# Emitting the late output matmuls of an RWKV scan ahead of the state's own update, and the merge of the solved triangles after the pair's last gate blocks

## The chip, the core and the metric

The kernel runs on one NeuronCore of a Trainium2 chip. The metric is the device time of one execution in microseconds (us). Before the change the median of three runs is 3319.86 us (3317.98 to 3334.59). The engines named below are TensorE (PE; its weight loads are listed apart as PEld), VectorE (DVE), ScalarE (ACT), GpSimd (POOL) and SyncE (SP), which issues the DMAs. Each works off its own list of instructions in order.

## The reference

One step of a two-layer model on 128 context and 512 latent tokens of width 1024, all in float32. The part that matters here is the RWKV-7 branch of each layer: 16 heads of 64, two scan directions, a 64x64 state per head and direction. The gates and both branches are then mixed.

```
def _rwkv_step(S, inp):
    r, w, k, v, neg_kk, b = inp
    sa = jnp.einsum('dbhij,dbhj->dbhi', S, neg_kk)
    S = S * w[..., None, :] + sa[..., :, None] * b[..., None, :] + v[..., :, None] * k[..., None, :]
    return S, jnp.einsum('dbhij,dbhj->dbhi', S, r)
...
    z = h @ p['w_in'][l]
    z_rwkv, z_u, z_v, z_ga, z_gb = jnp.split(
        z, [C_RWKV, C_RWKV + D_B, C_RWKV + 2 * D_B, C_RWKV + 2 * D_B + D_MODEL], axis=-1)
...
    y_a, S_fin = rwkv_branch(z_rwkv, S0, p, l)
    y_b = chunk_mlp_branch(z_u, z_v, p, l)
    mixed = (jax.nn.sigmoid(z_ga) * y_a + jax.nn.sigmoid(z_gb) * y_b) @ p['w_out'][l]
```

## The kernel before

The 640 tokens stand in the free dimension, the 1024 channels in eight blocks of 128 partitions. A pair is two heads, which is one such block, so a layer has eight pairs. The scan is done in chunks of 64 tokens, ten to a direction.

Every large product is a block of 48 dense matmuls (`mm_block`, L111): weights and activations are split into a high and a low part (`load_w`: SP loads the raw weights, ACT makes `hi` at L101, DVE or POOL makes `lo` at L103), and three products of 128x128 by 128x320 are summed per 128 rows. Of these there are three for each pair (`krv_block`: k, r and v) and 16 gate blocks (`gate_block`), which wait for nothing of the scan and are spread over the pairs by the numbers in `SP["gn"]`: two for most pairs, one for pairs 3 and 7, and two before the first.

For each pair there is a `front` and a `back`, both generators that emit their instructions up to the next `yield`. `front(i)` builds the chunk matrices LA and BK, their products `g` (L644), and then solves 40 small triangular systems with a chain of 60 DVE instructions on the tile X (L676 and L678). After that come two last parts. In the first, DVE transposes X into XT and XN (L692, L694) and ACT copies XT into TT (L698). In the second, the merge, 40 matmuls of 32x32 (`pw`, L705), four ACT copies (L709), 40 more matmuls of 32x32 (L715) and four more copies (L718) put the off-diagonal block into TT. `front` yields 22 times in all; the merge is what runs between the 21st and the 22nd.

`back(i)` is the recurrence: ten steps, each for both directions and heads. A step reads the state with LA (L776 for the part of the output, L751 for the solve's right-hand side), ACT copies the latter into `psb` (L780), four matmuls apply the solved triangle TT (L789), ACT and DVE copy the result into SV (L790, L791), four matmuls form the new state (L795), and two DVE additions put it into SV for the next step (L803). The last four matmuls of a step's output, `y_mm` (L757), are kept in `late` and emitted in the next step. They are followed by an addition on DVE (L764) or, where a token's output is written for the first time, a copy on ACT (L766). All of the step's matmuls are of 64 or 128 rows by 64 columns; two or four of them work side by side in the array.

The program's order is not what the code says alone. The recording layer gives each instruction a priority from its place of emission; `tc.high_priority(offset=n)` lets instructions count as if they were emitted n instructions earlier. A scheduler then goes through the program with its own reckoning of when things are ready, and puts on each engine's list the ready instruction of the highest priority. The engines work off those lists in order. `adv` takes the offset from the table SP: 200 for `front` ("F"), none for `back` ("B"). `run(i, n)` advances front i by up to n parts.

The functions that the change touches, and what calls them:

Of the kernel before, what the change touches and what calls it, by code (L numbers as in the profile page):

```python
# [31 lines left out]
DPAR = 27 + 16 + 16 + 8 + 8  # L32
SPLIT = (((0, NCH),), ((0, NCH),))
GORD = (((0, 4), (4, 4), (8, 2)), ((0, 4), (8, 2), (4, 4)))
SP = {'n': (3, 2, 1, 2, 2, 1, 0, 0, 3, 1), 'v': 1, 'k': 4, 'r': 7, 'kk': 7, 'F': 200, 'B': None, 't': 10, 'g0': 2, 'gn': (2, 2, 2, 1, 2, 2, 2, 1)}


def cidx(d, p):
# [3 lines left out]
def emit(tc, I, O, depth=DEPTH, mark=lambda s: None):  # L42
    nc = tc.nc
    ctx = ExitStack()
    with ctx:
# [261 lines left out]
        for l in range(depth):  # L307
# [73 lines left out]
            with tc.tile_pool(name=f"com{l}", bufs=1) as com:  # L381
# [11 lines left out]
                with tc.tile_pool(name=f"p1_{l}", bufs=1) as p1:  # L393
                    lah = p1.tile([128, 3, T], F32R, tag="lah", name="lah")
                    lal = p1.tile([128, 3, T], F32R, tag="lal", name="lal")
                    late = iter(range(16, 48 if l == 0 else 16))
# [7 lines left out]
                    for j in range(3):  # L404
# [9 lines left out]
                        t = p1.tile([128, T], F32, tag="pt", name="lz", bufs=4)  # L414
# [66 lines left out]
                    for q in range(4):  # L481
                        mod_some(0)
                        pss = [dense_ps(), dense_ps()]
                        for kb in range(4):
                            wh, wl = load_w(I["win"][l, 35 + 2 * q + kb // 2, :, (kb % 2) * 512:(kb % 2) * 512 + 512])
                            for kk in range(2):
                                k = 2 * kb + kk
# [33 lines left out]
                with tc.tile_pool(name=f"rw{l}", bufs=1) as rw:  # L521
# [199 lines left out]
                    def back(i):  # L721
# [3 lines left out]
                        for d in range(2):  # L725
                            for w0 in range(-1, NCH, 4):
                                tr = psr.tile([128, 4, 2, L], F32, tag="g", name="trv")
                                n = min(4, NCH - w0)
# [16 lines left out]
                        late = None  # L745

                        def y_state(pu, cs, us):
                            for d in range(2):
                                for h in range(2):
                                    s = slice(64 * h, 64 * h + 64)  # L750
                                    nc.tensor.matmul(pu[s, d, 3, :], SV[s, us[d], h, :], LA[d][s, cs[d], 1, :], start=False, stop=False, skip_group_check=True)  # L751

                        def y_mm(pu, cs, us):
                            for d in range(2):
                                for h in range(2):
                                    s = slice(64 * h, 64 * h + 64)
                                    nc.tensor.matmul(pu[s, d, 3, :], SV[:, us[d], h, :], GR[d][:, cs[d], h, :], start=False, stop=True, skip_group_check=True)  # L757
                            for d in range(2):
                                tok = cs[d] if d == 0 else NCH - 1 - cs[d]
                                dst = y[:, tok * L:(tok + 1) * L]  # L760
                                if d:
                                    dst = dst[:, ::-1]
                                if tok in seen:
                                    nc.vector.tensor_tensor(dst, pu[:, d, 3, :], dst, ALU.add)  # L764
                                else:
                                    nc.scalar.activation(dst, pu[:, d, 3, :], AF.Copy)  # L766
                                    seen.add(tok)

                        for p in [2, 0, 3, 1] + list(range(4, 10)):
                            cs = [cidx(d, p) for d in range(2)]  # L770
                            us = [cs[0], NCH + cs[1]]
                            both = slice(us[0], us[1] + 1, us[1] - us[0])
                            pu = psr.tile([128, 2, 4, L], F32, tag="pu", name="pu")
                            for d in range(2):
                                for h in range(2):
                                    nc.tensor.matmul(pu[64 * h:64 * h + 64, d, 0, :], LA[d][:, cs[d], 2 * h, :], SV[:, us[d], h, :],  # L776
                                                     start=(d == 0), stop=True, skip_group_check=True)
                            y_state(pu, cs, us)
                            psb = rw.tile([128, 2, L], F32, tag="psb", name="psb", bufs=2)
                            nc.scalar.activation(psb, pu[:, :, 0, :], AF.Copy)  # L780
                            if p != 9:
                                sw = rw.tile([128, 2, L], F32, tag="sw", name="sw", bufs=2)
                                for h in range(2):
                                    s = slice(64 * h, 64 * h + 64)
                                    nc.gpsimd.tensor_tensor(sw[s], SV[s, both, h, :], wcu[s, both].unsqueeze(2).to_broadcast([64, 2, L]), ALU.mult)  # L785
                            for d in range(2):
                                for h in range(2):
                                    s = slice(64 * h, 64 * h + 64)
                                    nc.tensor.matmul(pu[s, d, 1, :], TT[s, us[d], :], psb[s, d, :], start=False, stop=True, skip_group_check=True)  # L789
                            nc.scalar.activation(SV[0:64, both, 0, :], pu[0:64, :, 1, :], AF.Copy)  # L790
                            nc.vector.tensor_copy(SV[64:128, both, 1, :], pu[64:128, :, 1, :])  # L791
                            if p != 9:
                                for d in range(2):
                                    for h in range(2):
                                        nc.tensor.matmul(pu[64 * h:64 * h + 64, d, 2, :], BT[d][:, cs[d], h, :], SV[:, us[d], h, :], start=False, stop=True, skip_group_check=True)  # L795
                                for h in range(2):
                                    s = slice(64 * h, 64 * h + 64)
                                    if p == 1:
                                        dst = sw[s]
                                    else:  # L800
                                        v0, v1 = cidx(0, p + 1), NCH + cidx(1, p + 1)
                                        dst = SV[s, v0:v1 + 1:v1 - v0, h, :]
                                    nc.vector.tensor_tensor(dst, pu[s, :, 2, :], sw[s], ALU.add)  # L803
                                if p == 1:
                                    nc.sync.dma_start(O["st"][l, i], sw)
                            if late:
                                y_mm(*late)
                            late = (pu, cs, us)
                            yield "ch"
                        y_mm(*late)  # L810
# [23 lines left out]
                    def adv(g, what, i):  # L834
                        mark(f"{what}{i}:")
                        if SP[what] is None:
                            return next(g, None)
                        with tc.high_priority(offset=SP[what]):
                            return next(g, None)
# [13 lines left out]
                    def gate(n):  # L853
                        nonlocal gi
                        for _ in range(min(n, len(gates) - gi)):
                            mark("gate")
                            gate_block(*gates[gi])
                            gi += 1

                    def run(i, n=99):  # L860
                        f = fronts.get(i)
                        for _ in range(n):
                            if f is None or adv(f, "F", i) is None:
                                break

                    def branch_b():
# [27 lines left out]
                    for i in range(NPAIR):  # L894
                        ng = SP["gn"][i]
                        for step in range(10):
                            adv(b, "B", i)
                            run(i + 1, SP["n"][step])
                            if step == SP["v"]:
                                krv(i + 1, 2)  # L900
                            if step == SP["k"]:
                                krv(i + 2, 0)
                            if step == SP["r"]:
                                krv(i + 2, 1)
                            if step == SP["kk"]:
                                run(i + 2, 1)
                        gate(min(ng, 1))
                        if i == NPAIR - 1:
                            ya = new_acts()
                            for j in range(NPAIR - 1):  # L910
                                t = ftmp("ya")
                                nc.sync.dma_start(t, yd[j])
                                split(ya[0][:, j], ya[1][:, j], t)
                        drain(b, "B", i)
                        if i == NPAIR - 1:
                            branch_b()
                        gate(ng - 1)
                        run(i + 1)
                        if i + 1 < NPAIR:
                            b = back(i + 1)  # L920
                            adv(b, "B", i + 1)
                        run(i + 2, 4)

                mark("p3")
                with tc.tile_pool(name=f"x{l}", bufs=1) as xpool:
# [38 lines left out]
                    with tc.tile_pool(name=f"ff{l}", bufs=1) as ff:  # L964
# [3 lines left out]
                        for half in range(2):  # L968
                            fh = ff.tile([128, 16, T], F32R, tag="fh", name="fh")
                            fl_ = ff.tile([128, 16, T], F32R, tag="fl", name="fl")  # L970
                            for m in range(16):
# [6 lines left out]
                                t = ff.tile([128, T], F32, tag="nt", name="relu", bufs=3)  # L978
# [99 lines left out]
```

## Time and profile before

| | |
|---|---|
| median of three runs | 3319.86 us |
| profiled execution | 3320.89 us |
| its span, from the first to the last instruction | 3319.2 us |
| PE busy in the span | 3129.1 us (94%) |
| DVE busy | 2156.9 us (65%) |
| ACT busy | 1509.4 us (45%) |
| mean granted TensorE clock | 0.954 of 2.4 GHz |

The two stretches with the recurrence are 340 to 1055 us (layer 0) and 1960 to 2690 us (layer 1). PE is busy in most of both, DVE in four fifths. In a view of PE's timeline a row merges equal instructions that follow each other; a float32 matmul is listed as two passes, so the 40 `pw` matmuls of the program stand as x80, and a group of four state matmuls as x8. A dense matmul (L111) is listed once. The duration of a row reaches to the modelled end of its last matmul, which lies beyond the start of the next; the time that a matmul takes from PE is read from one start to the next.

### The profile page before, as it was taken

How to read it: one execution, taken by the hardware profiler on the slowest of the kernel's cores; microseconds unless marked ns; L12 is line 12 of the kernel's file. 1: busy time of each engine (PE TensorE's matmuls, PEld its weight loads, DVE VectorE, ACT ScalarE, POOL GpSimd, SP SyncE). 2: the span in 40 equal slices, each digit the busy share in tenths (PEclk: the TensorE clock that was granted, in tenths of full speed). 3: DMA queues.
4: the chain of work that ended last, by engine and by line, in shares of the span. 5: the costliest groups of instructions: out<-in, count | busy, mean ns of one | idle time of the engine just before them, and what ended most of it. 6: DMA issues, size and time to landing. Idle time of an engine off the chain costs nothing.

```text
span 3319.2 us, 66348 instructions
## 1 busy us (share of the span) xinstructions
PE 3129.1 (94%) x26160; PEld 2840.5 (86%) x26160; DVE 2156.9 (65%) x4147; ACT 1509.4 (45%) x3268; POOL 613.5 (18%) x616
## 2 busy tenths in 40 slices
PE   8999799999999999999999979999999999999998
PEld 7988677777778989999999967787777799899998
DVE  6777778878875468943363387788897735532334
ACT  5444444554555345224264434455554533541432
POOL 3004333333331010000010143333333200100000
PEclk7998889999999999999999989899999999999999
DMA  6683122222224626632344521122222345222223
GB/s 206 203 299 124 57 74 67 76 67 74 67 80 125 216 83 212 217 115 77 93 146 145 189 79 57 58 81 72 78 75 73 104 142 169 89 77 74 77 74 102
DMA packets 215671, 372.73 MB, mean 112 GB/s; under 512 B 63680, under 2 KB 72000, under 8 KB 215360
## 3 DMA queue, kind: packets, MB, share of 16 engines
q1 hardware_dynamic: 215360, 368.49, 34.7%
q8 instruction: 206, 3.38, 0.4%
q14 instruction: 105, 0.86, 0.1%
HBM read 288.41 MB, written 63.31 MB: 106 GB/s over the span
## 4 chain that ended last, share of the span: by engine, by line
PE 66%; DVE 18%; issue 5%; DMA 4%; ACT 4%; POOL 2%; SPq 0%; DVEq 0%; POOLq 0%; ACTq 0%
PE dps L111 43%; PE g L644 4%; DMA wada<-in_wada 3%; PE dps L491 3%; PE dps L256 3%; DVE D L676 2%; DVE X L678 2%; DVE wjunk L168 2%; PE pu L776 2%; PE pu L789 2%; PE pu L751 1%; PE pu L757 1%; PE pu L795 1%; DVE lo L103 1%; DVE XN L694 1%
## 5 line engine op out<-in xcount | busy, mean ns | idle before, releaser
L101 ACT ACTIVATE hi<-raw 128x512 fp32r<-128x512 f32 x630 | 396.2, 631 | 1006.6 <-PE dps L111 803.0
L103 DVE TENSOR_TENSOR lo<-raw,hi 128x512 fp32r<-128x512 f32 x550 | 393.9, 718 | 522.5 <-ACT hi L101 510.8
L111 PE MATMUL dps<-ah,hi 128*128 128x320 f32 x2768 | 685.2, 324 | 7.6 <-ACT up L468 4.1
L111 PE MATMUL dps<-ah,lo 128*128 128x320 f32 x2768 | 677.7, 321 | 0.0
L111 PE MATMUL dps<-al,hi 128*128 128x320 f32 x2768 | 677.6, 322 | 0.0
L111 PEld LDWEIGHTS dps<-ah,hi 128*128 128x128 f32 x2768 | 474.5, 192 | 26.7 <-ACT up L468 5.2
L111 PEld LDWEIGHTS dps<-ah,lo 128*128 128x128 f32 x2768 | 474.2, 192 | 14.5 <-issue 0.4
L111 PEld LDWEIGHTS dps<-al,hi 128*128 128x128 f32 x2768 | 475.0, 192 | 13.2 <-issue 0.4
L168 DVE CUSTOM_DVE_ANT_0 wjunk<-wada,sc 128x1024 f32<-128x1024 f32 x176 | 221.9, 1261 | 34.2 <-DMA wada<-in_wada 32.2
L785 POOL TENSOR_TENSOR sw<-SV,wc 64x128 f32<-64x128 f32 x288 | 150.6, 523 | 450.5 <-DVE SV L803 438.6
L644 PE MATMUL g<-LA,BK 64*128 64x128 f32 x1280 | 183.1, 315 | 34.2 <-POOL BK L625 13.4
L103 POOL TENSOR_TENSOR lo<-raw,hi 128x512 fp32r<-128x512 f32 x80 | 118.2, 1477 | 511.8 <-ACT hi L101 425.5
L111 PE MATMUL dps<-fh,lo 128*128 128x320 f32 x896 | 204.6, 310 | 3.4 <-DVE lo L103 3.4
L644 PEld LDWEIGHTS g<-LA,BK 64*128 64x128 f32 x1280 | 153.4, 211 | 62.2 <-issue 23.6
L111 PE MATMUL dps<-fh,hi 128*128 128x320 f32 x896 | 204.3, 309 | 0.0
L111 PE MATMUL dps<-fl,hi 128*128 128x320 f32 x896 | 204.1, 309 | 0.0
L676 DVE TENSOR_TENSOR D<-AA,X 128x30 f32<-128x30 f32 (+14 forms) x480 | 182.6, 380 | 24.3 <-POOL X L671 14.2
L678 DVE TENSOR_TENSOR X<-X,D 128x30 f32<-128x30 f32 (+14 forms) x480 | 176.3, 367 | 10.5
L249 POOL TENSOR_TENSOR al<-nt,ah 128x320 fp32r<-128x320 f32 x24 | 26.7, 1114 | 705.1 <-ACT ah L248 704.0
L625 POOL TENSOR_TENSOR BK<-ta,cum 64x640 f32<-64x640 f32 x64 | 128.3, 2004 | 139.2 <-DVE ta L616 108.3
L111 PEld LDWEIGHTS dps<-fh,lo 128*128 128x128 f32 x896 | 149.6, 188 | 4.7 <-DVE lo L103 4.7
L111 PEld LDWEIGHTS dps<-fl,hi 128*128 128x128 f32 x896 | 149.9, 188 | 0.0
(293 smaller groups left out, 5773.8 us busy)
## 6 DMA issues: line engine op xcount, KB each, us to landing
raw<-in_w SPq DMA_DIRECT2D x280, 256.0 KB, 2.6
raw<-in_win SPq DMA_DIRECT2D x234, 256.0 KB, 2.8
wada<-in_wada SPq DMA_DIRECT2D x88, 512.0 KB, 4.1
ld<-up SPq DMA_DIRECT2D x80, 320.0 KB, 3.5
th<-ld SPq DMA_DIRECT2D x32, 320.0 KB, 3.0
ta<-ld SPq DMA_DIRECT2D x32, 320.0 KB, 3.1
gd<-spill SPq DMA_DIRECT2D x32, 320.0 KB, 2.3
raw<-in_wo SPq DMA_DIRECT2D x40, 256.0 KB, 2.6
```

The source lines that it names most:

```text
L101: nc.scalar.activation(hi, raw, AF.Copy)
L103: (eng or nc.vector).tensor_tensor(lo, raw, hi.bitcast(F32), ALU.subtract)
L111: nc.tensor.matmul(ps[:, n, 0:HT], w[:, k * 128:(k + 1) * 128], xk[:, n * HT:(n + 1) * HT], start=(first and k == 0 and j == 0), stop=(las ...
L168: nc.vector.tensor_tensor_reduce(junk, wt, sc_cur[0][:, v, :], 1.0, 0.0, ALU.mult, ALU.add, mods[l][:, j, v:v + 1])
L256: nc.tensor.matmul(ps[:, n, 0:HT], w[:, k * 128:(k + 1) * 128], x[:, 4 * kb + k, hs(n)], start=(kb == 0 and k == 0 and j == 0), stop=(kb = ...
L491: nc.tensor.matmul(o, x[:, k, tk * 128:(tk + 1) * 128], w[:, kk * 256:(kk + 1) * 256], start=(k == 0 and j == 0 and tk % 2 == 0), stop=(k ...
L625: nc.gpsimd.tensor_tensor(b[s, c, 1 - h, :], rt[s], e[s], ALU.mult)
L644: nc.tensor.matmul(gs[h][:, c - c0, :], b[s, c, :, :].rearrange("p x t -> p (x t)"), la[s, c, h:h + 2, :].rearrange("p x t -> p (x t)"), s ...
L676: nc.vector.tensor_tensor(t3, AA[:, s + 1:32, s:s + 1].to_broadcast([128, n, s]), X[:, s:s + 1, 0:s].to_broadcast([128, n, s]), ALU.mult)
L678: nc.vector.tensor_tensor(X[:, s + 1:32, 0:s], X[:, s + 1:32, 0:s], t3, ALU.add)
L776: nc.tensor.matmul(pu[64 * h:64 * h + 64, d, 0, :], LA[d][:, cs[d], 2 * h, :], SV[:, us[d], h, :], start=(d == 0), stop=True, skip_group_c ...
L785: nc.gpsimd.tensor_tensor(sw[s], SV[s, both, h, :], wcu[s, both].unsqueeze(2).to_broadcast([64, 2, L]), ALU.mult)
```

## The change

Two edits. The call of `y_mm` for the step before moves from the end of a step to the place right behind `y_state`, ahead of the copy into `psb`. And at the end of a pair the first of the two last parts of the next front (transposes and copies) is emitted ahead of the pair's last gate blocks, still with an offset of 200, and the merge behind them, with a new offset of 60. No instruction is added or taken away on any engine: all five lists keep their counts by operation and shape.

```
-SP = {'n': (3, 2, 1, 2, 2, 1, 0, 0, 3, 1), 'v': 1, 'k': 4, 'r': 7, 'kk': 7, 'F': 200, 'B': None, 't': 10, 'g0': 2, 'gn': (2, 2, 2, 1, 2, 2, 2, 1)}
+SP = {'n': (3, 2, 1, 2, 2, 1, 0, 0, 3, 1), 'v': 1, 'k': 4, 'r': 7, 'kk': 7, 'F': 200, 'M': 60, 'B': None, 't': 10, 'g0': 2, 'gn': (2, 2, 2, 1, 2, 2, 2, 1)}
...
                             y_state(pu, cs, us)
+                            if late:
+                                y_mm(*late)
                             psb = rw.tile([128, 2, L], F32, tag="psb", name="psb", bufs=2)
...
                                     nc.sync.dma_start(O["st"][l, i], sw)
-                            if late:
-                                y_mm(*late)
                             late = (pu, cs, us)
...
-                    def run(i, n=99):
+                    def run(i, n=99, what="F"):
                         f = fronts.get(i)
                         for _ in range(n):
-                            if f is None or adv(f, "F", i) is None:
+                            if f is None or adv(f, what, i) is None:
...
                             branch_b()
+                        run(i + 1, 1)
                         gate(ng - 1)
-                        run(i + 1)
+                        run(i + 1, 9, "M")
                         if i + 1 < NPAIR:
```

The scheduler makes the following of it. On PE in layer 0, the merge of front 3 stood before as one run of 40 `pw` matmuls and then the second 40 in two runs, with state matmuls between them:

```order
L111 MATMUL dps<-al,hi 128x320
L705 MATMUL pw<-XN,TT_3559 32x32 x40
L776 MATMUL pu<-SV,LA_2793 64x64 x2
L776 MATMUL pu<-SV,LA_2815 64x64 x2
L751 MATMUL pu<-LA_2793,SV 64x64 x2
L751 MATMUL pu<-LA_2815,SV 64x64 x2
L757 MATMUL pu<-GR_2832,SV 64x64 x2
L757 MATMUL pu<-GR_2890,SV 64x64 x2
L111 MATMUL dps<-al,hi 128x320
L111 MATMUL dps<-ah,lo 128x320 x2
L715 MATMUL pw_6709<-XT,XN 32x32 x19
```

The same merge in the changed kernel, again on PE:

```order
L111 MATMUL dps<-al,hi 128x320 x2
L705 MATMUL pw<-XN,TT_3559 32x32 x16
L578 MATMUL pg<-YD,ones_b 128x320 x2
L705 MATMUL pw<-XN,TT_3559 32x32
L111 MATMUL dps<-ah,lo 128x320
L705 MATMUL pw<-XN,TT_3559 32x32
L111 MATMUL dps<-ah,lo 128x320
L705 MATMUL pw<-XN,TT_3559 32x32
L111 MATMUL dps<-ah,hi 128x320
L705 MATMUL pw<-XN,TT_3559 32x32
L111 MATMUL dps<-ah,hi 128x320
L111 MATMUL dps<-al,hi 128x320
```

After the first 16 the `pw` matmuls stand one at a time between dense matmuls; the first 40 of this merge are now in 23 pieces and the second 40 in 15.

The first edit shows on PE where a step stands among a `front`'s products. The piece is the difference between the two lists in layer 0, among the first steps of pair 0 (matmuls of L795 have the number L797 in the changed kernel):

```order
 L644 MATMUL g<-LA_3520,BK_3521 128x128 x4
-L795 MATMUL pu<-SV,BK_2794 64x64
-L795 MATMUL pu<-SV,BK_2816 64x64 x2
 L757 MATMUL pu<-GR_2832,SV 64x64 x2
 L757 MATMUL pu<-GR_2890,SV 64x64 x2
+L797 MATMUL pu<-SV,BK_2794 64x64
+L797 MATMUL pu<-SV,BK_2816 64x64 x2
```

The four output matmuls now stand ahead of the last three matmuls of the new state.

## Rows read from the trace of the kernel before

**Rows 1.** The page: busy time by engine, and the chain by engine.
```profile
PE 3129.1 (94%) x26160; PEld 2840.5 (86%) x26160; DVE 2156.9 (65%) x4147; ACT 1509.4 (45%) x3268; POOL 613.5 (18%) x616
...
PE 66%; DVE 18%; issue 5%; DMA 4%; ACT 4%; POOL 2%; SPq 0%; DVEq 0%; POOLq 0%; ACTq 0%
```
**Rows 2.** Windows of both recurrences: us, busy by engine, PEclk, DMA share, GB/s.
```profile
340.00:1055.00 715.00, 662.77 (x6962) 539.19 (x6963) 576.80 (x1229) 363.47 (x952) 239.87 (x246) 0.93 0.25 76
...
1960.00:2690.00 730.00, 674.69 (x7114) 548.79 (x7112) 589.28 (x1256) 368.78 (x961) 237.02 (x248) 0.94 0.25 76
```
**Rows 3.** PE's waits, whole span: total us, times, longest.
```profile
PE pw L705 <- DVE XN L694: 52.5, 16, 16.5
```
**Rows 4.** PE's waits, 440 to 1055 us (layer 0, fronts 1 to 7).
```profile
PE pw L705 <- DVE XN L694: 9.7, 7, 3.4
PE g L644 <- POOL wc L610: 3.5, 1, 3.5
PE g L644 <- DVE LA L656: 2.9, 5, 1.0
...
PE g L644 <- POOL BK L625: 2.0, 2, 1.4
```
**Rows 5.** PE's waits, 2060 to 2690 us (layer 1), those for `g`.
```profile
PE g L644 <- DVE LA L656: 4.5, 7, 1.3
...
PE g L644 <- POOL wc L610: 2.3, 1, 2.3
...
PE g L644 <- POOL BK L625: 1.2, 2, 1.0
```
**Rows 6.** PE's timeline around the merge of front 3, layer 0: start us, us.
```profile
630.40 0.46 PE L111 MATMUL dps<-ah,hi 128*128 128x320 f32 x2
...
632.46 0.31 PE L111 MATMUL dps<-al,hi 128*128 128x320 f32 x1
634.00 1.45 PE L705 MATMUL pw<-XN,TT 32*32 32x32 f32 x80 [1.23 <-DVE XN L694]
...
638.28 0.88 PE L715 MATMUL pw<-XT,XN 32*32 32x32 f32 x42
```
**Rows 7.** The same timeline, cut to single instructions at two borders.
```profile
636.92 0.31 PE L111 MATMUL dps<-ah,lo 128*128 128x320 f32 x1
637.16 0.31 PE L715 MATMUL pw<-XT,XN 32*32 32x32 f32 x8
...
638.97 0.19 PE L715 MATMUL pw<-XT,XN 32*32 32x32 f32 x1
639.09 0.41 PE L111 MATMUL dps<-ah,hi 128*128 128x320 f32 x1
```
**Rows 8.** PE's timeline in a step of pair 0, layer 0.
```profile
421.90 0.31 PE L111 MATMUL dps<-al,hi 128*128 128x320 f32 x1
422.14 0.33 PE L776 MATMUL pu<-SV,LA 128*64 128x64 f32 x2
422.40 0.42 PE L111 MATMUL dps<-al,hi 128*128 128x320 f32 x1
...
427.04 0.70 PE L578 MATMUL pg<-kksq,ones_b 128*128 128x320 f32 x2
427.34 0.55 PE L111 MATMUL dps<-ah,lo 128*128 128x320 f32 x1
```
**Rows 9.** PE's window behind the wait of front 2, layer 0: busy, PEclk.
```profile
555.20:558.60 3.40, 3.40 (x49) 0.50 0.51 153
```
**Rows 10.** PE's timeline in that window.
```profile
555.29 0.73 PE L111 MATMUL dps<-ah,hi 128*128 128x320 f32 x2
555.82 0.73 PE L111 MATMUL dps<-al,hi 128*128 128x320 f32 x2
```
**Rows 11.** ACT's copies on the recurrence: duration ns min/median/max.
```profile
L766 ACT ACTIVATE YD<-pu x160: 197/224/245, 394.2 to 2669.2; 128x64 f32<-128x64 f32 x160
...
L780 ACT ACTIVATE psb<-pu x160: 250/278/283, 384.8 to 2683.0; 128x128 f32<-128x128 f32 x160
```

## The prediction

> **What bounds the kernel now.** I read the busy times first. PE is busy 94% of the span and makes up 66% of the chain that ended last [rows 1], so what PE does more, or waits less, is worth about its own time as long as nothing else takes over. The change touches the two recurrences alone, and so the windows of these came next: PE is busy 662.8 of 715 us and 674.7 of 730 us there, DVE 577 and 589 [rows 2]. PE is the fuller engine, and DVE has a fifth to spare. Then PE's waits, to see what the change could take away: the longest group is the merge's first matmul (L705) waiting for DVE's second transpose, 52.5 us in 16 waits [rows 3]. Of these 9.7 us are those of fronts 1 to 7 in layer 0 [rows 4], and layer 1 shows the same sum. The other 33.1 us belong to the first front of each layer, which has no gate blocks in the place that the change uses. So the second edit can win 19.4 us of waiting at most. Last I compared PE's two lists, since a wait that goes is replaced by what stands there instead.
>
> **The first edit.** It adds nothing; the four output matmuls, the addition and the copy of each step only move. On PE they stood directly behind L751, where the edit asks for them, in 84 of 160 steps before, and do in 92 after; behind the state's update (L795) they stood in 36 and stand in 28. The scheduler had filled this place already, and I cost the edit on PE at nothing; what hides it are the dense matmuls around each step. On ACT it adds a wait. In 28 steps, against 6 before, a copy of the output (L766) now stands right ahead of the copy into `psb` (L780), and that waits for two copies of 0.224 us [rows 11] and for the output matmuls before them. Behind `psb` come TT's matmuls (L789). 22 steps by 0.45 us is 10 us on the recurrence's own chain, but a dense matmul or two stand ahead of L789 in each step, as in the step shown [rows 8]. I take 2 us. No DMA is moved by it.
>
> **The second edit, what it takes away.** The wait at the merge goes only if PE has more to do ahead of it. For front 1 of layer 0, whose wait is the longest, 3.4 us [rows 4], 64 dense matmuls stood between the last group-norm product (L578) and the merge; now it is 59, at 0.147 us each (14 starts from 630.40 to 632.46 [rows 6]). For front 2 the count from there falls from 41 to 19, with two more L578 among them, while DVE has three products fewer and one half of the group norm more ahead of the transposes. For front 3 the merge moves behind the step's end on both engines. The scheduler believes XN ready sooner than it is, in both kernels, and puts the merge where it believes so. I take 5 of the 19.4 us as won, with 0 and 19.4 as the ends.
>
> **The second edit, what it adds.** With the offset of 60 the merge's matmuls have nearly the priority of the dense ones beside them, and the list takes them in turn. The first 40 of the 16 merges stood in 16 pieces and now stand in 202; the second 40 went from 20 pieces to 108. Counting over PE's whole list, it goes from matmuls that fill the array (128 rows by 128 columns) to smaller ones and back 639 times before and 871 times after: 232 more.
>
> The price of one such visit is in the trace. From a dense matmul to the first `pw` pass is 0.24 us (636.92 to 637.16), from the last pass back to a dense one 0.12 us (638.97 to 639.09) [rows 7], and a pass within a run takes 0.017 us (638.28 to 638.97 for 41 [rows 6, 7]). A lone `pw`, two passes, thus takes 0.24 + 0.017 + 0.12 = 0.377 us from one dense matmul to the next, where 0.147 us would pass without it and 0.034 us is what it costs within a run. That leaves 0.196 us for each visit, and 232 of them make 45.5 us. From below, an instruction of another line between dense ones that fills the array costs nothing but its passes: L578 takes 0.30 us for two passes of 320 columns, 0.006 us over two dense ones. From above, a lone L776 takes 0.50 us from dense to dense, 0.35 over [rows 8]. The ends are 1 and 82 us. I take 45.5, since the borders priced are those of these very instructions.
>
> The Trainium skill, on its page "TensorEngine Tiling (Array Packing)", section "Tiling Modes" (Key Properties), says that changing the tiling mode drains the engine; the 0.24 and 0.12 us agree. The same page, section "Performance Considerations" (Instruction Overhead), gives a matmul about 60 cycles of overhead; if that were all, my estimate at 2.4 GHz would be 232 x 0.025 = 6 us, and the sum would end 39.5 us lower, at 3313 us.
>
> What hides a part of it: after each merge PE waits for LA, BK and `wc` of the next front before its products `g`, 8.4 us in layer 0 and 8.0 in layer 1 [rows 4, 5]. Where PE is late anyway, these waits shrink. But the exponentials on ACT that DVE and POOL need for them now stand behind copies that wait for the stretched merge (L709), as do casts of the weights (L101; four buffers of `hi` are the cover, 24 dense matmuls each). I take 10 of the 16.4 us as hidden. The gate blocks' loads and stores on SP are the same number, and no DMA stands among the releasers of PE's waits in these two lists [rows 4, 5].
>
> **Sum.** 45.5 - 10 - 5 + 2 = 32.5 us on the profiled 3320.89 us, which is 3353.4. The median of the runs shown is 1.03 us under that execution, so 3352 us.
>
> **Rivals.** About 0.5%, 17 us, is what a measurement of this kernel can tell from no change; faster means under 3303 and slower over 3336 us.
>
> A second price, the clock. Behind the wait of front 2 the granted clock is 0.50 for 3.4 us [rows 9], 1.2 GHz, and a dense matmul takes 0.265 us [rows 10]. A stretch of lone matmuls gives PE little work in its time too, 232 x 0.377 = 87 us in all. If it all ran at the low level at up to 1.8 times the time, that is 70 us more; a third of it makes 23 us and 3375 us. For it speaks that the mean clock is 0.93 and 0.94 in just these two windows [rows 2]; against it, that the recurrence's steps, full of borders too, run at the full clock: the step shown enters L776 in 0.24 us [rows 8], as a dense matmul is left in rows 7.
>
> No change. The visits cost 45.5 us, but all of the waits for `g` and at the merge fill up: 45.5 + 2 - 19.4 - 16.4 = 12 us, 3331 us. The merges stand next to just these waits, which speaks for it; the lists, which put no more ahead of the merge than before, speak against it.
>
> Faster. A lone `pw` fits between dense matmuls at little over its passes, as L578 does: 1 us. The waits at the merges go (19.4), and with them four stretches like that of rows 9, 1.7 us lost in each, 7 us: 1 + 2 - 19.4 - 7 = -23, 3297 us. It decides as soon as a visit costs less than (19.4 + 7 - 2) / 232 = 0.105 us. The rule of 60 cycles cited above from the Trainium skill would lead here. Against it stand 0.24 and 0.12 us, read at those instructions. That the second edit does nothing is excluded by the lists; that the first does nothing is what I forecast.
>
> **How the numbers follow.** The forecast has a chance of 0.58, and its own range is 3337 to 3372 us (10 us hidden may be 0 to 16.4, 5 won may be 19.4, and 0.196 may be 0.25). The clock has 0.15, no change 0.17, faster 0.10. For 8 in 10 the range goes from 3316 to 3388 us, which leaves out the faster case and the clock's far end. Slower by over 0.5%: nearly all of the forecast and the clock, 0.70. Within: no change, a little of the forecast and a part of the faster case, 0.23. Faster: 0.07.
>
> **What would show it.** In the changed profile, PE's lone L705 between two L111 should take 0.37 to 0.38 us from dense to dense; if it is 0.2, the main term is wrong. PE's waits at L705 should still sum to over 40 us (33.1 of the first fronts, and most of 19.4); if under 36, the edit did win them. The waits for `g` should fall by half. The windows of the two recurrences should be 16 us longer each, and all others the same. PEclk below 0.90 in these windows would be the rival of the clock. The forecast is wrong as a whole if these windows grow by less than 5 us each.

## The result and the profile after

The changed kernel takes 3445.86 us (median of 6 runs, 3429.19 to 3459.31) where the kernel before takes 3329.81 us (6 runs, the three of its table among them): a ratio of 1.035, 95% interval 1.0319 to 1.0381. That it would be slower was forecast, the size was not: 116 us measured against 32.5 forecast, and outside the range.

The lines of the page that answer to [rows 1]:

```profile
PE 3268.5 (95%) x26160; PEld 2907.9 (85%) x26160; DVE 2160.5 (63%) x4147; ACT 1507.1 (44%) x3268; POOL 600.7 (17%) x616
...
PE 74%; DVE 14%; DMA 4%; issue 4%; ACT 3%; POOL 1%; SPq 0%; DVEq 0%; POOLq 0%; ACTq 0%
```

PE is busy for 139 us more with the same 26160 instructions, while DVE, ACT and POOL are busy about as long as before. So the same matmuls take PE longer. To find the place, each trace is read from the first matmul of a layer's first merge to that of its last. The columns are those of [rows 2]; first the kernel before, then the changed one:

```profile
369.82:1009.66 639.84, 604.99 (x6283) 491.95 (x6283) 520.97 (x1129) 322.31 (x863) 225.92 (x229) 0.94 0.23 70
1994.66:2629.68 635.02, 600.34 (x6284) 488.46 (x6284) 523.58 (x1129) 322.12 (x863) 222.26 (x229) 0.94 0.23 71
```

```profile
364.35:1056.62 692.27, 666.41 (x6245) 521.73 (x6245) 523.66 (x1127) 319.32 (x859) 217.87 (x227) 0.89 0.21 65
2047.33:2747.80 700.47, 673.92 (x6246) 523.75 (x6248) 522.90 (x1127) 319.17 (x859) 215.83 (x227) 0.88 0.21 64
```

The stretches grow by 52.4 and 65.5 us, 117.9 of the span's 121.3 (3440.5 against 3319.2). The granted clock in them falls from 0.94 to 0.89 and 0.88. PE's busy time in them grows by 61.4 and 73.6 us, 135.0 in all; its idle time, which is the rest of a stretch, falls from 69.5 us in the two to 52.4. Within them, four of the merges of layer 0 (fronts 3 to 6) from the first `pw` to the end of the second 40, PE's columns and PEclk again; before, then after:

```profile
634.00:639.09 5.09, 5.09 (x196) 4.50 (x196) 2.83 (x7) 3.76 (x10) 2.19 (x3) 1.00 0.41 119
731.68:735.90 4.22, 4.22 (x169) 3.99 (x169) 2.11 (x5) 3.16 (x8) 0.42 (x1) 1.00 0.22 58
829.91:835.90 5.99, 5.99 (x171) 5.62 (x171) 5.92 (x9) 3.80 (x9) 0.42 (x1) 0.72 0.21 59
916.67:922.10 5.43, 5.43 (x196) 4.66 (x196) 1.61 (x5) 4.39 (x11) 1.22 (x3) 1.00 0.18 61
```

```profile
633.96:663.74 29.78, 29.78 (x206) 18.31 (x206) 16.89 (x20) 9.03 (x17) 6.25 (x5) 0.69 0.09 29
743.12:761.80 18.68, 18.68 (x215) 12.55 (x215) 5.14 (x12) 5.31 (x12) 2.77 (x4) 0.63 0.25 82
847.61:868.50 20.89, 20.89 (x194) 13.55 (x194) 14.08 (x16) 9.14 (x17) 6.35 (x5) 0.73 0.06 18
945.20:981.80 36.60, 36.60 (x218) 22.39 (x216) 17.06 (x21) 8.63 (x16) 6.68 (x5) 0.65 0.19 60
```

20.7 us have become 106 us, with 833 matmul passes where there were 732, and PE is never idle in them by the profile. Much of the clock's loss is here too: 0.63 to 0.73 where the whole stretch has 0.89. Single rounds in the merge of front 3 (PE's timeline, start and length), first at the full clock and then at the low one:

```profile
636.55 0.42 PE L111 MATMUL dps<-ah,lo 128*128 128x320 f32 x1
636.89 0.24 PE L705 MATMUL pw<-XN,TT 32*32 32x32 f32 x2
637.07 0.41 PE L111 MATMUL dps<-ah,hi 128*128 128x320 f32 x1
...
653.58 0.64 PE L111 MATMUL dps<-ah,hi 128*128 128x320 f32 x1
654.15 0.31 PE L715 MATMUL pw<-XT,XN 32*32 32x32 f32 x2
654.39 0.64 PE L111 MATMUL dps<-al,hi 128*128 128x320 f32 x1
```

From dense to dense it is 0.52 us at 636.55 and 0.81 us at 653.58, where I had forecast 0.377. Last, PE's waits at the merges of fronts 1 to 7 and for the products `g`, layer 0 and then layer 1, which answer to [rows 4] and [rows 5]:

```profile
PE pw L705 <- DVE XN L694: 8.7, 6, 3.4
PE g L644 <- DVE LA L656: 4.0, 6, 1.6
...
PE g L644 <- POOL BK L625: 1.8, 2, 1.2
```

```profile
PE pw L705 <- DVE XN L694: 8.7, 6, 3.3
PE g L644 <- DVE LA L656: 4.3, 7, 1.6
...
PE g L644 <- POOL BK L625: 0.3, 1, 0.3
```

At the merges that is 17.4 us where it was 19.4: the wait that the second edit was placed to fill is still there. The waits for LA, BK and `wc` are 10.4 us where they were 16.4.

### The profile page after: what moved, and what is told of

Same layout as the page of the kernel before. It is cut to its first block, busy times and chain, and to the rows that moved or that the text cites. A ratio compares the mean times of both kernels' runs of the same rounds, so it can differ in the third digit from the quotient of the medians.

```text
span 3440.5 us, 66359 instructions
## 1 busy us (share of the span) xinstructions
PE 3268.5 (95%) x26160; PEld 2907.9 (85%) x26160; DVE 2160.5 (63%) x4147; ACT 1507.1 (44%) x3268; POOL 600.7 (17%) x616
## 4 chain that ended last, share of the span: by engine, by line
PE 74%; DVE 14%; DMA 4%; issue 4%; ACT 3%; POOL 1%; SPq 0%; DVEq 0%; POOLq 0%; ACTq 0%
PE dps L111 47%; PE g L644 4%; DMA wada<-in_wada 3%; PE dps L491 3%; PE dps L256 2%; PE pu L776 2%; DVE wjunk L168 2%; PE pu L791 2%; PE pu L757 2%; PE pw L705 2%; DVE D L676 2%; PE pg L578 2%; DVE X L678 2%; PE pu L751 1%; PE pu L797 1%
## 5 line engine op out<-in xcount | busy, mean ns | idle before, releaser
L111 PE MATMUL dps<-ah,hi 128*128 128x320 f32 x2768 | 712.5, 332 | 7.8 <-ACT up L468 4.9
L111 PE MATMUL dps<-ah,lo 128*128 128x320 f32 x2768 | 711.2, 331 | 0.0
L103 DVE TENSOR_TENSOR lo<-raw,hi 128x512 fp32r<-128x512 f32 x550 | 382.5, 697 | 510.8 <-ACT hi L101 494.3
L111 PE MATMUL dps<-al,hi 128*128 128x320 f32 x2768 | 702.7, 329 | 0.0
L111 PEld LDWEIGHTS dps<-ah,hi 128*128 128x128 f32 x2768 | 481.6, 195 | 32.4 <-ACT up L468 5.9
L111 PEld LDWEIGHTS dps<-ah,lo 128*128 128x128 f32 x2768 | 485.2, 195 | 18.0 <-issue 1.5
L111 PEld LDWEIGHTS dps<-al,hi 128*128 128x128 f32 x2768 | 482.5, 195 | 16.5 <-issue 0.6
L111 PEld LDWEIGHTS dps<-fh,hi 128*128 128x128 f32 x896 | 149.8, 188 | 0.0
```

Of the source, the lines that this page charges most:

```text
L103: (eng or nc.vector).tensor_tensor(lo, raw, hi.bitcast(F32), ALU.subtract)
L111: nc.tensor.matmul(ps[:, n, 0:HT], w[:, k * 128:(k + 1) * 128], xk[:, n * HT:(n + 1) * HT], start=(first and k == 0 and j == 0), stop=(las ...
```

## The experiments

Theory 1 was that the lost time is PE's price for going from dense matmuls to a small one and back, with the clock that falls where it does so often. Theory 2 was that the merge, and with it the next recurrence, simply comes later. Theory 3 laid it to the first edit. How late a merge comes can be counted in the traces, in passes of PE's other matmuls ahead of it, here for layer 0 (layer 1 has the same differences): against the kernel before, the change starts it later in fronts 3 and 6 only (4200 and 6452 passes, before 4141 and 6414), and ends it later in fronts 1, 3, 4, 5 and 6. Visits are counted over PE's list as in the prediction: 639 before, 871 in the changed kernel.

**The first edit alone.** The last part of a pair is put back:

```
-                        run(i + 1, 1)
                         gate(ng - 1)
-                        run(i + 1, 9, "M")
+                        run(i + 1)
```

> Only the first edit (output matmuls ahead of psb); the merge as before. PE's list has 631 visits to smaller matmuls, 8 fewer than before (639; the changed kernel has 871). Theory 1 (the time is PE's price for the extra visits, plus the clock that falls in them): ratio to before 0.995 to 1.003, and PEclk of the recurrences 0.92 or more. Theory 2 (the merge comes late and the recurrence waits for it): also about 1.00, since the merge is not moved. Theory 3 (the copies of the output that stand ahead of psb on ScalarE slow the recurrence): about 1.035, as the whole change.

Measured: 3322.95 us against 3330.04, ratio 0.9985 (0.9963 to 1.0006). Theory 3 falls: the first edit can't be told from no change.

**The second edit alone.** The call of `y_mm` is put back behind the state's update.

> Only the second edit (merge behind the gate blocks with offset 60); the output matmuls as before. 877 visits, 238 more than before. Theory 1: 238 by 0.5 us each (116 us over 232 visits in the whole change) is 119 us, ratio 1.036, and PEclk 0.87 to 0.90 in the recurrences. Theory 2: 1.035 as well. Theory 3: 1.00.

Measured: 3458.65 us, ratio 1.0394 (1.0359 to 1.0429), and 0.926 for the mean clock of the span. All of the loss is in the second edit; 128.6 us over 238 visits is 0.54 us for each.

**The merge in the change's place, but whole.** The change, with each 40 matmuls of a merge tied to the first of them. The helper `keep` issues the first as the change does and the other 39 behind it at a high priority:

```
...
+                        def keep(f):
+                            if not head:
+                                head.append(f())
+                            else:
+                                with tc.issue_after(head[0].ins), tc.high_priority(offset=1000):
+                                    f()
...
```

> The whole change, but each 40 matmuls of a merge are kept together: the first of them has the offset of 60 and its place, the other 39 follow it at a high priority. 633 visits. Theory 1: ratio 0.99 to 1.005, PEclk 0.92 or more, since all the extra visits are gone though the merge starts as late as in the change. Theory 2: 1.02 to 1.035, since the merge starts at its late place. Theory 3: 1.035.

Measured: 3334.5 us, ratio 1.0015 (0.9991 to 1.0039), mean clock 0.949. The merge starts within 29 passes of where it starts in the change, and nothing is lost. What costs is that the merge stands in pieces. For Theory 2 this run is not enough: a whole merge also ends earlier, in front 3 after 4194 other passes where it was 4246.

**No offset for the merge.** One number is changed in the changed kernel: `'M': 60` becomes `'M': None`.

> The whole change with no offset for the merge in place of 60: the merge's matmuls then stand behind nearly all of the gate block's, later than in the change, in 22 pieces each for the first and the second 40; 623 visits, 16 fewer than before. Theory 1: ratio 0.985 to 1.00 (16 visits fewer, and the first matmul of a merge waits less for the transposes). Theory 2: slower than the change, 1.035 to 1.05, since the merge is later still. Theory 3: 1.035.

Measured: 3299.12 us, ratio 0.9916 (0.9883 to 0.9949). In fronts 2 to 6 the merge starts and ends later than in the change, in few pieces, and the kernel is faster than before. Theory 2 falls here. PE's busy time and, over the whole span, the wait at the merge's first matmul and two waits of the transposes `trv` behind the merge, which load SV for the next pair:

```profile
PE 3101.2 (94%) x26160; PEld 2817.9 (86%) x26160; DVE 2157.1 (66%) x4147; ACT 1507.6 (46%) x3268; POOL 605.3 (18%) x616
...
PE pw L705 <- DVE XN L694: 39.3, 8, 16.0
...
PE trv L730 <- ACT TT L718: 13.7, 14, 2.6
PE trv L730 <- ACT SV L735: 10.0, 6, 4.4
```

At the merge that is 13.2 us less than the 52.5 of [rows 3], and 8 waits where there were 16. But the two waits of `trv` were 2.3 and 1.1 us before:

```profile
PE trv L730 <- ACT TT L718: 2.3, 6, 0.5
...
PE trv L730 <- ACT SV L735: 1.1, 7, 0.2
```

PE's idle time in the span is 192.0 us where it was 190.1, so the gain is not there; it is in the 27.9 us by which PE is busy less. 16 visits fewer are about 5 us of that at the price found below; the mean clock is 0.959 where it was 0.954, and how the rest divides is open.

**An offset between.** `'M': 100`.

> The whole change with an offset of 100 for the merge in place of 60: 767 visits, 128 more than before, where the change has 232 more. Theory 1: 128/232 of 116 us, 64 us, ratio 1.019; 1.012 to 1.027. A rival by which any offset under 200 that lets the merge mix costs the same: 1.035.

Measured: 3397.37 us against 3325.75, ratio 1.0213 (1.0189 to 1.0236). 71.6 us over 128 visits is 0.56 us for each, as in the second edit alone (0.54) and the whole change (116 over 232, 0.50). Over these three the time goes with the number of visits.

**The price by itself.** Here small matmuls are added to the kernel before, in the feed-forward part of layer 1 where PE has nothing but dense work. Their result is not used. `small` issues one, in turn in two places of the array, and stands behind every dense matmul of seven blocks:

```
+            tc.keep_in_program_order(nc.tensor.matmul(lone[0][64 * h + 32:64 * h + 64, 0:32], ident[q, 0:32], ident[q, 0:32], start=True, stop=True))
...
                             start=(first and k == 0 and j == 0), stop=(last and k == 3 and j == 2))
+                        if lone[0] is not None and n >= 0:
+                            small()
```

> The kernel before with 336 matmuls of 32x32 added in the second layer's first feed-forward half, where PE does nothing but dense matmuls: one behind every dense matmul of seven blocks. Their result is not used. Theory 1, with the durations read at the changed kernel's lone merge matmuls (0.34 us into it, 0.053 for its two passes, 0.12 out, where 0.147 would pass): 336 by 0.37 us is 124 us if the clock stays full; if it falls to the low level in that stretch, 0.81 us a round, 336 by 0.66 us, 222 us. The price as predicted (0.24 us in) would give 336 by 0.23 us, 77 us. Rival: a small matmul between dense ones costs only its passes, under 15 us, and the lost time in the changed kernel came from waits around the merge.

Measured: 3551.87 us (two runs), 226 us more, ratio 1.0677 (1.0634 to 1.0721). PE's timeline where the stretch begins and in its middle (L119 is the dense matmul here, `lone` the small one), and then windows of the stretch and of the dense work after it, with PEclk behind the five engines:

```profile
2887.52 0.41 PE L119 MATMUL dps<-ah,hi 128*128 128x320 f32 x1
2887.86 0.24 PE L111 MATMUL lone<-ident 32*32 32x32 f32 x2
2888.03 0.41 PE L119 MATMUL dps<-al,hi 128*128 128x320 f32 x1
...
3000.38 0.64 PE L119 MATMUL dps<-ah,lo 128*128 128x320 f32 x1
3000.95 0.31 PE L111 MATMUL lone<-ident 32*32 32x32 f32 x2
3001.19 0.64 PE L119 MATMUL dps<-ah,hi 128*128 128x320 f32 x1
```

```profile
2891.00:3156.00 265.00, 265.00 (x987) 152.66 (x986) 14.53 (x21) 21.94 (x33) 0.00 (x0) 0.50 0.05 14
3160.00:3300.00 140.00, 140.00 (x956) 140.00 (x956) 39.65 (x65) 39.80 (x61) 0.00 (x0) 1.00 0.24 74
```

The first rounds take 0.51 us; then the clock falls, each takes 0.81 us, and it stays low for all 265 us until the dense work after it. 336 rounds by 0.81 - 0.147 us are 223 us: there is no merge here, and PE is listed as busy for all of the 265 us, so no wait for another engine has a part in it.

The same number behind every second dense matmul (`n >= 1`, 14 blocks):

> As the run before, but the same 336 small matmuls stand behind every second dense matmul of 14 blocks; their result is not used. Theory 1: with two dense matmuls between them the way in costs 0.24 us, not 0.34, as in the trace of the kernel before: 336 by 0.27 us is 89 us at the full clock, and the clock stays full more of the time, since dense work fills more than half of the round. If the way in costs 0.34 us here too: 336 by 0.37, 124 us.

Measured: 3454.34 us (two runs), 129 us more, ratio 1.0384 (1.0345 to 1.0423). The same two views of it:

```profile
3000.17 0.56 PE L119 MATMUL dps<-ah,hi 128*128 128x320 f32 x2
3000.66 0.24 PE L111 MATMUL lone<-ident 32*32 32x32 f32 x2
3000.83 0.56 PE L119 MATMUL dps<-al,hi 128*128 128x320 f32 x2
```

```profile
2885.80:3107.00 221.20, 221.20 (x1343) 144.13 (x1342) 31.73 (x43) 49.27 (x73) 0.00 (x0) 1.00 0.11 36
```

The clock stays full. A round is 0.66 us (3000.17 to 3000.83) where two dense matmuls take 0.294: 0.37 us more, 123 us over 336 rounds. I had expected that two dense matmuls between visits make each cheaper, 89 us; they don't. The way in is 0.24 us then, but the first dense matmul after a visit takes 0.25 us instead of 0.147 (3000.17 to 3000.66 is 0.49 for both). With one dense matmul between visits the same 0.1 us shows as a way in of 0.34 us.

And 48 in a row behind each of seven blocks:

> The same 336 small matmuls as in the runs that priced them (result not used), but 48 in a row behind each of seven blocks, so 7 visits. If a visit's price lies in the way in and out: 7 by 0.33 us and 336 by 0.034 to 0.053 us, 14 to 20 us, ratio 1.004 to 1.006, and the clock stays full. If the price lies in each small matmul: over 89 us, as measured between dense ones.

Measured: 3343.42 us against 3329.28, ratio 1.0043 (1.0021 to 1.0065), 14 us for the same 336 matmuls.

```profile
2895.30 0.46 PE L119 MATMUL dps<-ah,lo 128*128 128x320 f32 x2
2895.69 1.71 PE L111 MATMUL lone<-ident 32*32 32x32 f32 x96
2897.33 0.57 PE L119 MATMUL dps<-ah,hi 128*128 128x320 f32 x2
```

From the first of 48 small matmuls to the next dense one it is 1.64 us here (2895.69 to 2897.33). The price is the visit's, not the small matmul's. Which part of a passage takes the time, the change of the array's use or the load of other weights, these runs do not separate.

**What is best.** With no offset and whole runs:

> The whole change with no offset for the merge and each 40 of its matmuls kept together. 617 visits, 22 fewer than before and 6 fewer than with no offset alone; all 32 groups of 40 in one piece. Theory 1: 6 visits by 0.5 us are 3 us: ratio 0.985 to 0.993, the same as or slightly under the run with no offset alone (0.9916). Theory 2 is out already.

Measured: 3309.36 us against 3325.75, ratio 0.9952 (0.9926 to 0.9977), faster than before but outside what I had expected; keeping the runs whole wins nothing over no offset. Then no offset again, in five more runs:

> The version with no offset once more (whole change, merge without offset), in five rounds, for its interval: ratio 0.988 to 0.995 as before. If the first result was chance, 0.995 to 1.00.

Measured: 3299.16 us against 3329.28, ratio 0.9915 (0.9884 to 0.9947). And no offset without the first edit:

> The second edit alone with no offset; the output matmuls as before. 629 visits, 10 fewer than before. If the gain of the version with no offset comes from the merge's place (its first matmul waits 8 us in fronts 1 to 7 of both layers, where it waited 19.4): 0.988 to 0.996. If it needs the first edit: 0.997 to 1.002.

Measured: 3300.0 us, ratio 0.9916 (0.9884 to 0.9948). No offset beats both kernels by itself; the first edit adds nothing that can be told. The wait at the merge's first matmul, over the whole span:

```profile
PE pw L705 <- DVE XN L694: 37.6, 6, 16.5
```

## Why the prediction was wrong

The prediction had the cause, and two terms of its second edit were wrong: the price of a visit, and the clock, which stood in the sum at nothing.

**The first edit** was costed at nothing on PE and 2 us on ACT. Measured alone it is 0.9985; right, as far as this can tell.

**The count of visits** was right as a cause: the loss follows it over four kernels (0, 128, 232 and 238 more visits, 0, 72, 116 and 129 us). Small differences do not follow it: 16 visits fewer went with 31 us less, 22 fewer with 16.

**The price of one such visit** is the first step that failed. I put it at 0.377 us from dense to dense and 0.196 us net, from the borders of a run. Those borders are right, 0.24 us in and 0.12 us out, but they are not all of a visit: the first dense matmul after one takes 0.1 us more, and a lone small matmul's own two passes 0.053 us, not the 0.017 of a run. A round takes 0.516 us at the full clock, 0.335 us net (less 0.147 and 0.034). 232 of those are 78 us where I had 45.5. [Rows 8] had shown 0.35 us for a lone state matmul, and the trace of the kernel before has 52 such rounds at the full clock, with a median of 0.35. I kept that for the upper end and trusted the cheaper reading because it was of the same instructions, though at the end of a run of 42 and not of a lone one.

**The clock** is the second step that failed, and the larger one. It was a rival with a chance of 0.15 in place of a term of the sum, and its 23 us were too little. The sign named for it, PEclk below 0.90 in the two stretches, came: 0.89 and 0.88. Of the 230 rounds in the trace with a dense matmul on both sides of a lone one, 145 ran wholly at the low level, 73 at the full one and 12 across a change. At 0.626, 0.335 and about 0.45 us net they make 90.8 + 24.5 + 5.4 = 121 us, 43 us over the 78 at the full clock. That is most of the 135.0 us by which PE's busy time grew in the two stretches; the other 14 us I have not assigned. I had weighed that the recurrence's steps keep the full clock although they are full of borders. The trace of the kernel before says so in one place and not in another. Two windows of its first layer, PE and PEclk, the second behind a wait of 1.7 us:

```profile
400.00:450.00 50.00, 49.05 (x467) 1.00 0.19 57
...
473.30:504.00 30.70, 30.64 (x184) 0.50 0.19 67
```

In the first the steps stand among dense matmuls. In the second they stand among the products `g`, with few dense ones, and the clock is at the low level for all of it though PE is listed as busy for 30.64 of 30.70 us. So the reason against the rival did not hold, and the trace that I had could have shown it.

**What the second edit takes away** was forecast as 5 of 19.4 us at the merges; it was 2.0. The reason held: in most fronts the scheduler put the merge no later among PE's other matmuls. With no offset it did, and there these waits fell by 13 us, but those of `trv` took their place.

**The 10 us hidden** behind waits for the next front are in part there: the waits for `g` that the sum had in view fell by 6.0 us. All of PE's idle time in the two stretches fell by 17.1 us, near the 10 + 5 of the sum, though not all in the places named; that the two totals agree is in part luck. So the stretches grew by 117.9 us and not by 135.0.

The Trainium skill's page "TensorEngine Tiling (Array Packing)", "Tiling Modes" (Key Properties), with its drain at a change of mode, agrees with the runs of 336 small matmuls, in which 336 visits cost 129 us at the full clock and 7 visits with as many matmuls 14 us, though no run shows that it is a drain. The estimate of 6 us from the 60 cycles of overhead on the same page does not agree.

## What to carry to other kernels

Small packed matmuls belong in runs: on PE each passage from matmuls over the whole array to a small one and back costs about a third of a microsecond here at the full clock (0.37 us for a lone matmul of 32x32, 0.35 for a lone state matmul) and 0.66 at the low one, so a list with an instruction in turn from each of two streams is the worst mix of them. When a priority is changed, count in the built order how often an engine changes its kind of work, beside what it waits for: an offset of 60 and no offset at all ended 4% apart. And price an event from a place where it happens alone, over a whole round, and not by adding its borders.

## What the runs showed of the hardware

The granted clock fell and stayed at 0.50 (1.2 GHz) for 265 us in which PE, by the profile, was busy all of the time, with one dense matmul of 320 columns and one small one in turn; with two dense matmuls to each small one it stayed at 1.00 for 221 us. The sum of the prediction had no fall but those behind waits; only its rival of the clock had one among lone matmuls. The Trainium skill's page "TensorE: Matmul & The Clock Gate", Part 1, says that activity releases the throttle and idleness brings it back; here a change in what PE did was enough, with no wait listed, and a share of busy time in the profile does not tell of it. The ends of matmuls are modelled in the profile, so pauses inside that busy time are not excluded.
